# Layer norm in a two-layer encoder: statistics by products with a constant matrix of 1/D, and 1/std by square root, reciprocal and one Newton step

## The chip, the cores and the metric

The kernel runs on one core of a Trainium2 chip. The metric is device time in microseconds (us) of one execution. The core's engines run side by side, each through its own instructions in order: TensorE (PE in the profile: matmuls; PEld: its weight loads), VectorE (DVE), ScalarE (ACT), GpSimd (POOL) and SyncE (SP, which issues the DMAs here). An instruction that waits for another engine also holds back what stands behind it on its own engine.

## The reference

The program is two layers of a hybrid encoder over 1024 prompt tokens and 32 sample tokens, with D = 1024 features and a feed-forward width of 2816. Each layer has an input projection, mixers (pooling and a short convolution in layer 0, spatial gating and a state-space scan in layer 1), an output projection, and then three steps:

```python
x = layer_norm(alpha * x + mix, ln1_g, ln1_b)                                    # LN1
x = layer_norm(alpha * x + (silu(x @ w1) * (x @ w3)) @ w2, ln2_g, ln2_b)         # LN2
x = x + (ple[i] @ w_ple) * jax.nn.sigmoid(x @ w_gate)

def layer_norm(x, g, b, eps=1e-5):
    mu = jnp.mean(x, -1, keepdims=True)
    var = jnp.mean(jnp.square(x - mu), -1, keepdims=True)
    return (x - mu) * lax.rsqrt(var + eps) * g + b
```

All numbers are float32. The statistics of a layer norm are per token, over its 1024 features.

## The kernel before, in words

**Layout.** Activations lie with features on the 128 partitions: 8 blocks of 128 features by 1056 tokens (`stream`). A sum over features is therefore a sum over 8 blocks, which VectorE can do, and a sum over 128 partitions, which only a matmul does here. Tokens are cut in two ways: into three chunks of 384, 384 and 288 (named 0, 1, 2) or into two halves of 528 (t = 0, 1).

**Products.** Each big product is made of parts: an operand is split into a high part (`xhin`, `xhgate`; ScalarE, L323) and the rest (`xlin`, `xlgate`; VectorE, L324), and TensorE does three products, high by high, high by low and low by high (L228 to L230). From L990 on, and at L1203, a block-wise scheme with fewer products is used, on `quads` (PSUM tiles of two halves of 264 columns).

**Order.** Python code emits the work of each engine, and a list scheduler in the compiler then puts each engine's instructions in an order; at run time that order is fixed. To lay small steps under big products, the code calls `defer(us, fn)`: it counts the columns given to TensorE as time, and emits `fn` once that many microseconds of products have been passed. Those waits are the constants `LN_A` (before the first step of a norm), `LN_S` (between the two statistics), `LN_B` (before the result is applied), `LN_C` and `LN_D` (between the pieces in which it is applied).

**Where the norm stands.** `norm()` is called ten times, at two kinds of place.

- LN1, on chunks (`rows` is None), three times in each layer, in the function `tail` of a layer. The output projection (`down`: products L228 to L230, results added to `stream` by VectorE at L1282, `evacuate`) goes chunk by chunk. After every second feature block, `sums` squares that part (ScalarE) and adds it to S and Q (VectorE, L1394, L1395; at the end L1399): 128 partial sums of z and z*z for each token. When a chunk is done, its norm runs under the products of the next chunk; then it gives the chunk's operands `xhin` and `xlin`, in four pieces of two feature blocks. Behind chunk 2 of `down` the first products of the feed-forward (`up` of its first group, again L228 to L230, chunk after chunk, into `c`, L886) take these operands: they run while the norms of chunks 1 and 2 are still under way. After them the block-wise products at L990 begin.
- LN2, on halves (`rows` given), twice in each layer. t = 0 begins in the last products of the feed-forward (L1203) and lies under the 192 products with `w_ple` (L1310, whose results ScalarE copies out at L1315); these do not need its result. The gate's products (L1331, sigmoid at L1337) do need it: their operands `xhgate` and `xlgate` are this norm's output, in four pieces. t = 1 lies under the gate's products for t = 0.

**The norm itself.** `stats` multiplies S, as the stationary operand, 128 tokens at a time, by a column of 1/D (`rD`), and Q likewise: mean and mean square stand on the partitions, one token each, 3 or 5 columns (L1412). Small VectorE operations make the variance (L1425 to L1429). GpSimd raises it to the power -0.5 (L1430), multiplies the mean by the result (L1431), and builds diagonal matrices from both (`dg`, L1441). `spread` multiplies these by a matrix of ones (`cst`), so that 1/std and mean/std of every token stand on all partitions (L1456); on halves ScalarE copies them out of PSUM (L1468). Then, in each of four pieces, VectorE multiplies by 1/std (L1479) and subtracts mean/std (L1480), ScalarE applies gain and bias (L1482), and the piece is split (L323, L324).

Of the kernel before, what the change touches and what calls it, by code (L numbers as in the profile page):

```python
# [7 lines left out]
F32 = mybir.dt.float32  # L8
# [6 lines left out]
P = 128  # L15
# [18 lines left out]
LN_A, LN_B, LN_C, LN_D, LN_S = 4.0, 5.0, 2.0, 4.0, 1.0  # L34
# [164 lines left out]
class Kernel:  # L199
# [50 lines left out]
    def build(self):  # L250
        nc, tc, a = self.nc, self.tc, self.a
        with ExitStack() as ctx:
# [34 lines left out]
            self.rD = const.tile([P, 1], F32, name="rD")  # L287
            nc.vector.memset(self.rD, 1.0 / D)
# [979 lines left out]
    def norm2(self, layer, t):  # L1268

        tok = slice(t * TH, (t + 1) * TH)  # L1270
        x = [v[:, :, tok] for v in (self.xh, self.xl)]
        self.norm(
            2 * layer + 1, t, [self.row(i) for i in (0, 2)], self.stream[:, :, tok], x, TH, self.done2,
            0, [self.row(i) for i in (8, 10, 22, 23, 4, 6)],
        )
# [104 lines left out]
    def sums(self, ln, c, i, S):  # L1380
# [19 lines left out]
        return out[:, 0, :], Q[:, 0, :]  # L1400

    def norm(self, ln, c, S, acc, x, n, done, wait=LN_A, rows=None):

        nc, lp = self.nc, self.hp if rows else self.lp

        full = n // P
        tiles = [i * P for i in range(full)] + [n - P] * (n % P > 0)
        nt = len(tiles)

        def stats(st, i):  # L1410
            for j, o in enumerate(tiles):
                nc.tensor.matmul(  # L1412
                    st[:, nt * i + j:nt * i + j + 1], S[i][:, o:o + P], self.rD, start=True, stop=True
                )

        def first():
            st = self.quads()[:, 0, :] if rows else self.bank("ms")
            stats(st, 0)
            self.defer(LN_S, lambda: second(st))

        def second(st):
            stats(st, 1)
            sm = lp.tile([P, 2, nt], F32, tag="sm", name=f"sm{ln}_{c}", bufs=2)
            rn = lp.tile([P, 2, nt], F32, tag="rn", name=f"rn{ln}_{c}", bufs=2)
            nc.vector.tensor_copy(sm.rearrange("p a b -> p (a b)"), st[:, 0:2 * nt])  # L1425
            mean, var = sm[:, 0, :], sm[:, 1, :]
            nc.vector.tensor_tensor(rn[:, 0, :], mean, mean, op=ALU.mult)
            nc.vector.tensor_tensor(var, var, rn[:, 0, :], op=ALU.subtract)
            nc.vector.tensor_scalar(out=var, in0=var, scalar1=0.0, scalar2=EPS, op0=ALU.max, op1=ALU.add)  # L1429
            nc.gpsimd.tensor_tensor(rn[:, 0, :], var, self.mhalf[:, 0:nt], op=ALU.pow)  # L1430
            nc.gpsimd.tensor_tensor(rn[:, 1, :], mean, rn[:, 0, :], op=ALU.mult)  # L1431

            dg = []
            for i in range(2):
                for j in range(0, nt, 3):
                    k = min(3, nt - j)
                    if rows:
                        d = rows[len(dg) + 2][:, :k * P]
                    else:
                        d = lp.tile([P, 3 * P], F32, tag=f"dg{i}", name=f"dg{ln}_{c}_{i}", bufs=1)  # L1440
                    nc.gpsimd.tensor_tensor(  # L1441
                        d.rearrange("p (a t) -> p a t", a=k), self.ident.unsqueeze(1).to_broadcast([P, k, P]),
                        col(rn[:, i, j:j + k], P), op=ALU.mult,
                    )
                    dg.append(d)
            self.defer(LN_B, lambda: apply([dg[:len(dg) // 2], dg[len(dg) // 2:]]))

        def spread(ps, dg, t, end):

            t0 = t  # L1450
            while t < end:
                tail = t >= full * P
                j = full if tail else t // P
                upto = min(end, n if tail else min(full, j // 3 * 3 + 3) * P)
                o = t - tiles[j] + j % 3 * P
                nc.tensor.matmul(  # L1456
                    ps[:, t - t0:upto - t0], self.ones, dg[j // 3][:, o:o + upto - t], start=True, stop=True
                )
                t = upto

        def apply(dg):
            ab = []
            for i in range(2):
                if rows:
                    q = self.quads()
                    for a in range(2):
                        spread(q[:, a, :], dg[i], a * n // 2, (a + 1) * n // 2)
                    nc.scalar.activation(rows[i].rearrange("p (a t) -> p a t", a=2), q[:, :, :n // 2], AF.Copy)  # L1468
                    ab.append(rows[i])
                else:  # L1470
                    ps = self.bank("ms")
                    spread(ps, dg[i], 0, n)
                    ab.append(ps[:, :n])
            pieces([v.unsqueeze(1).to_broadcast([P, 2, n]) for v in ab], 0)

        def pieces(ab, k):
            ks = slice(k, k + 2)
            z = acc[:, ks, :]
            nc.vector.tensor_tensor(z, z, ab[0], op=ALU.mult)  # L1479
            nc.vector.tensor_tensor(z, z, ab[1], op=ALU.subtract)  # L1480
            for kk in (k, k + 1):
# [3 lines left out]
                )  # L1485
            self.split(x, ks, z)
            done[c] += 1
            if k + 2 < KD:
                self.defer(LN_D if rows else LN_C, lambda: pieces(ab, k + 2))
# [118 lines left out]
```

## Time and profile before

| | before |
|---|---|
| median of 3 runs | 2334.34 us (2331.43 to 2335.2) |
| the profiled execution | 2331.33 us |
| its span in the trace | 2329.6 us, granted TensorE clock 0.998 |
| TensorE busy | 2307.0 us, 99% of the span |
| VectorE busy | 1543.4 us, 66% |
| ScalarE busy | 966.1 us, 41% |
| GpSimd busy | 71.4 us, 3% |
| DMA | 207.37 MB moved, mean 89 GB/s |

The span is the time from the first to the last instruction in the trace; the profiled execution took 1.7 us more than that. Busy times add up the instructions of an engine; a busy TensorE still includes matmuls that wait in its pipeline. In the rows, `L1203 PE MATMUL q<-w 128*128 128x264 f32` is the instruction of line 1203 on TensorE that writes tile `q` from tile `w`, with its shapes; "x12" is how many, and in the chain of waits the numbers ahead are when a piece of the chain began and how long it lasted. Tile names are those under which a buffer was first made, and buffers are used again: `t1down` and `t2down` hold this norm's diagonals on halves, S and Q of a half among others, and `cst` holds the matrix of ones.

### The profile page before, as it was taken

The numbers are of one execution on the slowest core, as the hardware profiler recorded it, in microseconds if no ns is written. First come the engines' busy times: TensorE is split into PE (matmuls) and PEld (weight loads), VectorE is DVE, ScalarE is ACT, GpSimd is POOL, SyncE is SP. The second block draws the span as 40 slices with busy tenths as digits, with TensorE's granted clock in tenths as the row PEclk, the third lists the DMA queues.
The fourth block names the chain that finished last, engine by engine and source line by source line (L and its number), as shares of the span: only waits on it lengthen the run. The fifth ranks groups of instructions, "written<-read, shape, count | busy, mean of one in ns | idle before, by whom it ended". The sixth has DMA issues, their size and how long they took to land.

```text
span 2329.6 us, 41097 instructions
## 1 busy us (share of the span) xinstructions
PE 2307.0 (99%) x17567; PEld 2273.9 (98%) x17567; DVE 1543.4 (66%) x2426; ACT 966.1 (41%) x1616; POOL 71.4 (3%) x88
## 2 busy tenths in 40 slices
PE   9999999999999999999999999999999999999998
PEld 8999999999999999999999989999999999999998
DVE  8755787544554978775556774787554454978773
ACT  5432354333333444474543562353333333434462
POOL 0000000000000000100000120100000000000100
PEclk9999999999999999999999999999999999999999
DMA  4113123222224621124212222022222225521132
GB/s 148 47 55 127 39 68 107 74 83 74 92 73 151 239 88 44 46 83 141 80 38 66 100 85 61 19 89 94 84 73 89 73 69 205 215 69 42 37 102 91
DMA packets 84378, 207.37 MB, mean 89 GB/s; under 512 B 10236, under 2 KB 19652, under 8 KB 84196
## 3 DMA queue, kind: packets, MB, share of 16 engines
q1 hardware_dynamic: 83428, 204.07, 26.5%
q8 instruction: 137, 2.24, 0.4%
q10 hardware_dynamic: 768, 0.68, 0.1%
q14 instruction: 45, 0.37, 0.1%
HBM read 171.57 MB, written 33.16 MB: 88 GB/s over the span
## 4 chain that ended last, share of the span: by engine, by line
PE 94%; DVE 3%; DMA 1%; POOL 1%; ACT 1%; issue 0%; SPq 0%; POOLq 0%; ACTq 0%
PE q L990 38%; PE q L1203 20%; PE q L1331 8%; PE mm L228 6%; PE mm L229 6%; PE mm L230 6%; PE q L1310 2%; PE mm L639 1%; PE mm L640 1%; PE mm L641 1%; DVE bf L94 1%; PE ms L775 1%; DVE w L89 1%; DMA raw<-w_out 1%; DMA raw<-w 0%
## 5 line engine op out<-in xcount | busy, mean ns | idle before, releaser
L1203 PE MATMUL q<-w 128*128 128x264 f32 x3696 | 457.0, 285 | 0.0
L1203 PEld LDWEIGHTS q<-w 128*128 128x128 f32 x3696 | 456.1, 188 | 0.0
L88 ACT ACTIVATE w<-raw 128x512 fp32r<-128x512 f32 (+2 forms) x246 | 185.7, 774 | 221.1 <-issue 76.3
L990 PE MATMUL q<-xhin,w 128*128 128x264 f32 x1664 | 270.7, 284 | 2.0 <-ACT xhin L963 0.8
L89 DVE TENSOR_TENSOR w<-raw,w 128x512 fp32r<-128x512 f32 (+2 forms) x246 | 212.8, 878 | 55.1 <-ACT w L88 54.8
L89 DVE TENSOR_TENSOR w<-bf,w 128x512 fp32r<-128x512 f32 (+1 forms) x250 | 167.0, 691 | 106.7 <-ACT w L88 105.5
L990 PEld LDWEIGHTS q<-xhin,w 128*128 128x128 f32 x1664 | 230.1, 188 | 3.0 <-ACT xhin L963 1.0
L88 ACT ACTIVATE w<-bf 128x512 fp32r<-128x512 f32 (+1 forms) x250 | 149.0, 629 | 195.9 <-PE q L990 77.9
L990 PE MATMUL q<-xhgate,w 128*128 128x264 f32 x1280 | 207.9, 284 | 0.6 <-DVE c L886 0.6
L228 PE MATMUL mm<-xhgate,w 128*128 128x384 f32 (+1 forms) x576 | 187.5, 326 | 1.1 <-ACT xhgate L323 1.1
L230 PE MATMUL mm<-xlgate,w 128*128 128x384 f32 (+1 forms) x576 | 186.1, 324 | 0.0
L229 PE MATMUL mm<-xhgate,w 128*128 128x384 f32 (+1 forms) x576 | 185.9, 323 | 0.0
L990 PEld LDWEIGHTS q<-xhgate,w 128*128 128x128 f32 x1280 | 176.8, 188 | 1.0 <-issue 0.8
L990 PE MATMUL q<-xlin,w 128*128 128x264 f32 x832 | 169.9, 285 | 0.6 <-DVE xlin L964 0.6
L1331 PE MATMUL q<-xhgate,w 128*128 128x264 f32 x1024 | 166.7, 285 | 0.0
L1331 PEld LDWEIGHTS q<-xhgate,w 128*128 128x128 f32 x1024 | 141.6, 188 | 0.0
L990 PE MATMUL q<-xlgate,w 128*128 128x264 f32 x640 | 130.0, 285 | 0.4 <-DVE xlgate L964 0.4
L990 PEld LDWEIGHTS q<-xlin,w 128*128 128x128 f32 x832 | 128.8, 188 | 1.3 <-DVE xlin L964 1.0
L228 PE MATMUL mm<-xhin,w 128*128 128x384 f32 (+1 forms) x384 | 125.5, 328 | 3.0 <-ACT w L88 1.8
L229 PE MATMUL mm<-xhin,w 128*128 128x384 f32 (+1 forms) x384 | 124.2, 325 | 0.6 <-DVE w L89 0.6
L94 DVE TENSOR_TENSOR bf<-raw 128x512 f32<-128x512 f32 x50 | 34.5, 691 | 135.8 <-DMA raw<-w 129.8
L230 PE MATMUL mm<-xlin,w 128*128 128x384 f32 (+1 forms) x384 | 123.9, 325 | 0.0
(329 smaller groups left out, 4305.7 us busy)
## 6 DMA issues: line engine op xcount, KB each, us to landing
raw<-w SPq DMA_DIRECT2D x116, 512.0 KB, 3.6
hidden<-c SPq DMA_DIRECT2D x44, 528.0 KB, 3.0
raw<-w_gate SPq DMA_DIRECT2D x32, 512.0 KB, 3.6
raw<-w_in SPq DMA_DIRECT2D x16, 512.0 KB, 3.8
raw<-w_out SPq DMA_DIRECT2D x16, 512.0 KB, 3.6
xhdown<-hidden SPq DMA_DIRECT2D x12, 528.0 KB, 7.7
t2down<-hidden SPq DMA_DIRECT2D x8, 528.0 KB, 3.8
t3down<-hidden SPq DMA_DIRECT2D x8, 528.0 KB, 3.9
```

The source lines that it names most:

```text
L88: self.nc.scalar.activation(hi, x, AF.Copy)
L89: self.nc.vector.tensor_tensor(lo, x, hi.bitcast(F32), op=ALU.subtract)
L94: self.nc.vector.tensor_tensor(t, a, b, op=op)
L228: nc.tensor.matmul(ps, wh, xh, start=first, stop=False)
L229: nc.tensor.matmul(ps, wl, xh, start=False, stop=False)
L230: nc.tensor.matmul(ps, wh, xl, start=False, stop=last)
L639: nc.tensor.matmul(o, xh, hi[:, s], start=k == 0, stop=False)
L640: nc.tensor.matmul(o, xh, lo[:, s], start=False, stop=False)
L990: nc.tensor.matmul(ps[:, a, :TH // 2], w[q][:, ks], x[r][:, k, a * TH // 2:(a + 1) * TH // 2], start=not add and k == 0 and j == 0, stop=k ...
L1203: nc.tensor.matmul(ps[m][:, a, :TH // 2], v[q][:, ms], x[r][:, a * TH // 2:(a + 1) * TH // 2], start=j == 0 and n == 0, stop=j == NG - 1 a ...
L1310: nc.tensor.matmul(ps[:, b, :TH // 2], w[q][:, o:o + P], pe[k][r][:, t * TH + b * TH // 2:t * TH + (b + 1) * TH // 2], start=k == 0 and i ...
L1331: nc.tensor.matmul(ps[:, b, :TH // 2], w[q][:, ks], token_half((self.xh, self.xl), k, t, b)[r], start=k == 0 and i == 0, stop=k == KD - 1 ...
```

## The change

What changes:

- The matrix of ones is multiplied once, at the start, by 1/D. A product of it with S or Q then gives the mean, or the mean square, of each token on every partition at once (`average`). On chunks it is one product of 384 or 288 columns for each of the two, on halves two products of 264 columns for each.
- ScalarE copies the mean out of PSUM and squares it (L1431, L1432 of the new code). VectorE makes the variance (L1437, L1438), now 128 partitions by 384, 288 or 528 elements, ScalarE takes the square root (L1439, with a load of its table of functions), VectorE the reciprocal (L1444), and a Newton step follows: square (ScalarE, L1445), times the variance (VectorE, L1451), times -0.5 plus 1.5 (ScalarE, L1452), times the reciprocal (VectorE, L1457).
- The mean is subtracted from the four pieces of z in between (VectorE, L1427), before the multiplication by 1/std (L1463); each piece still has two VectorE operations for this, a gain and bias (L1465), and a split (L322, L323). `LN_B`, which stood once in a norm with 5.0, now stands three times with 2.0.
- GpSimd has no part in it any more: the power, the mean/std and the diagonals are gone, and so are the small statistics products and the products that spread them.

```diff
-LN_A, LN_B, LN_C, LN_D, LN_S = 4.0, 5.0, 2.0, 4.0, 1.0
+LN_A, LN_B, LN_C, LN_D, LN_S = 4.0, 2.0, 2.0, 4.0, 1.0
...
-            self.rD = const.tile([P, 1], F32, name="rD")
-            nc.vector.memset(self.rD, 1.0 / D)
+            nc.vector.tensor_scalar(out=self.ones, in0=self.ones, scalar1=1.0 / D, scalar2=None, op0=ALU.mult)
...
-        return out[:, 0, :], Q[:, 0, :]
+        return out, Q
...
+        if rows:
+            mean, var, inv, tmp = (r[:, :n] for r in rows[:4])
+        else:
+            mean, inv = (
+                lp.tile([P, 384], F32, tag=f"dg{i}", name=f"dg{i}_{ln}_{c}", bufs=2)[:, :n] for i in range(2)
+            )
+            var, tmp = S[0][:, 1, :], S[0][:, 0, :]
+
+        def average(v):
+            v = v if rows else v[:, 0, :]
+            if not rows:
+                ps = self.bank("ms")
+                nc.tensor.matmul(ps[:, :n], self.ones, v, start=True, stop=True)
+                return ps[:, :n], lambda t: t
+            q, h = self.quads(), n // 2
+            for a in range(2):
+                nc.tensor.matmul(q[:, a, :h], self.ones, v[:, a * h:(a + 1) * h], start=True, stop=True)
+            return q[:, :, :h], lambda t: t.rearrange("p (a t) -> p a t", a=2)
+
+        def minus(k):
+            z = acc[:, k:k + 2, :]
+            nc.vector.tensor_tensor(z, z, mean.unsqueeze(1).to_broadcast([P, 2, n]), op=ALU.subtract)
 
         def first():
-            st = self.quads()[:, 0, :] if rows else self.bank("ms")
-            stats(st, 0)
-            self.defer(LN_S, lambda: second(st))
...
-            nc.gpsimd.tensor_tensor(rn[:, 0, :], var, self.mhalf[:, 0:nt], op=ALU.pow)
-            nc.gpsimd.tensor_tensor(rn[:, 1, :], mean, rn[:, 0, :], op=ALU.mult)
...
+            ps, cut = average(S[0])
+            nc.scalar.activation(cut(mean), ps, AF.Copy)
+            nc.scalar.activation(cut(tmp), ps, AF.Square)
+            self.defer(LN_S, second)
+
+        def second():
+            ps, cut = average(S[1])
+            nc.vector.tensor_tensor(cut(var), ps, cut(tmp), op=ALU.subtract)
             nc.vector.tensor_scalar(out=var, in0=var, scalar1=0.0, scalar2=EPS, op0=ALU.max, op1=ALU.add)
+            nc.scalar.activation(tmp, var, AF.Sqrt)
+            minus(0)
+            self.defer(LN_B, third)
+
+        def third():
+            nc.vector.reciprocal(inv, tmp)
+            nc.scalar.activation(tmp, inv, AF.Square)
+            minus(2)
+            self.defer(LN_B, fourth)
+
+        def fourth():
 
+            nc.vector.tensor_tensor(tmp, tmp, var, op=ALU.mult)
+            nc.scalar.activation(tmp, tmp, AF.Copy, scale=-0.5, bias=1.5)
+            minus(4)
+            self.defer(LN_B, fifth)
+
+        def fifth():
+            nc.vector.tensor_tensor(inv, inv, tmp, op=ALU.mult)
+            pieces(0)
+
+        def pieces(k):
             ks = slice(k, k + 2)
             z = acc[:, ks, :]
-            nc.vector.tensor_tensor(z, z, ab[0], op=ALU.mult)
-            nc.vector.tensor_tensor(z, z, ab[1], op=ALU.subtract)
+            nc.vector.tensor_tensor(z, z, inv.unsqueeze(1).to_broadcast([P, 2, n]), op=ALU.mult)
...
+            if k == 0:
+                minus(6)
```

Below are two places at which the order of the instructions changes. A row names line, operation, tiles (with the number of their buffer) and shape. Elsewhere, outside the norms, every engine runs the same instructions in the same order, except that ScalarE has 46 loads of its function table in place of 33, for the square roots among its other functions.

TensorE in layer 0, at the end of the feed-forward (L1203) and the start of the `w_ple` products (L1310), where the norm of half t = 0 stands. Before, the ten small statistics products (`rD`) come first, and after three groups of `w_ple` products TensorE comes to the eight products that spread 1/std (from `t1down`) and mean/std (from `t2down`):

```order
L1412 MATMUL q_10109<-rD,t2down_7482 128x1 x5
L1203 MATMUL q_9782<-w_10008 128x264 x6
L1203 MATMUL q_9782<-w_10037 128x264 x6
L1310 MATMUL q_10168<-c0p,w_10078 128x264 x6
L1310 MATMUL q_10168<-w_10071,w_10078 128x264 x6
L1310 MATMUL q_10182<-c0p,w_10078 128x264 x6
L1310 MATMUL q_10182<-w_10071,w_10078 128x264 x6
L1310 MATMUL q_10196<-c0p,w_10078 128x264 x6
L1310 MATMUL q_10196<-w_10071,w_10078 128x264 x6
L1456 MATMUL q_10209<-t1down_7550,cst 128x264
L1456 MATMUL q_10209<-t1down_7550,cst 128x120
```

The same place of the changed kernel, where lines of the code are numbered one less:

```order
L1422 MATMUL q_10085<-t2down_7458,cst 128x264 x2
L1202 MATMUL q_9757<-w_9984 128x264 x5
L1202 MATMUL q_9757<-w_10013 128x264 x6
L1422 MATMUL q_10102<-t2down_7458,cst 128x264 x2
L1202 MATMUL q_9758<-w_9984 128x264 x6
L1202 MATMUL q_9758<-w_10013 128x264 x6
L1309 MATMUL q_10133<-c0p,w_10054 128x264 x6
L1309 MATMUL q_10133<-w_10047,w_10054 128x264 x6
L1309 MATMUL q_10150<-c0p,w_10054 128x264 x6
L1309 MATMUL q_10150<-w_10047,w_10054 128x264 x6
```

The four products that average stand where the statistics stood, among the last products of the feed-forward, and no product among those with `w_ple` belongs to the norm any more.

VectorE in the tail of layer 0, while TensorE does chunk 2 of `down`. Before, the norm of chunk 0 hands out its last operands (`xlin`), chunk 2 is taken in (L1282, L1394, L1395), and the norm of chunk 1 starts on its pieces with its 1/std and mean/std read from PSUM (`ms`):

```order
L1282 TENSOR_TENSOR stream<-stream,mm_2781 128x288
L1394 TENSOR_TENSOR S_2_1_2740<-S_2_1_2740,stream 128x2x288
L1395 TENSOR_TENSOR Q_2_0_2683<-Q_2_0_2683,sq_2_2_2777 128x2x288
L324 TENSOR_TENSOR xlin<-stream,xhin 128x2x384
L1479 TENSOR_TENSOR stream<-stream,ms_2808 128x2x384
L1282 TENSOR_TENSOR stream<-stream,mm_2795 128x288
L1480 TENSOR_TENSOR stream<-stream,ms_2810 128x2x384
L1394 TENSOR_TENSOR S_2_1_2740<-S_2_1_2740,stream 128x2x288
```

The same stretch of the changed kernel; `dg_0_1_2637` is the mean of chunk 1, `dg_0_1_2638` its 1/std, and `dg_0_0_2491` the 1/std of chunk 0:

```order
L1393 TENSOR_TENSOR S_2_1_2721<-stream 128x2x288
L1394 TENSOR_TENSOR Q_2_0_2674<-Q_2_0_2674,sq_2_1_2719 128x2x288
L1463 TENSOR_TENSOR stream<-stream,dg_0_0_2491 128x2x384
L1444 RECIPROCAL dg_0_1_2638<-S_1_1_2562 128x384
L323 TENSOR_TENSOR xlin<-stream,xhin 128x2x384
L1427 TENSOR_TENSOR stream<-stream,dg_0_1_2637 128x2x384
L1281 TENSOR_TENSOR stream<-stream,mm_2738 128x288
L1281 TENSOR_TENSOR stream<-stream,mm_2764 128x288
L1393 TENSOR_TENSOR S_2_1_2721<-S_2_1_2721,stream 128x2x288
L1394 TENSOR_TENSOR Q_2_0_2674<-Q_2_0_2674,sq_2_2_2760 128x2x288
L1463 TENSOR_TENSOR stream<-stream,dg_0_0_2491 128x2x384
L1451 TENSOR_TENSOR S_1_1_2562<-S_1_1_2562 128x384
```

Chunk 1's reciprocal, subtraction and Newton product now stand between the last two pieces of chunk 0, ahead of chunk 0's last operands and of the intake of chunk 2 (L1281).

More of the change, by code (lines that the diff above doesn't have):

```diff
@@ L1273, in norm2 @@
             2 * layer + 1, t, [self.row(i) for i in (0, 2)], self.stream[:, :, tok], x, TH, self.done2,
-            0, [self.row(i) for i in (8, 10, 22, 23, 4, 6)],
+            0, [self.row(i) for i in (8, 10, 4, 6)],
         )
@@ L1399, in sums @@
             nc.vector.tensor_tensor(v[:, 0, :], v[:, 0, :], v[:, 1, :], op=ALU.add)
-        return out[:, 0, :], Q[:, 0, :]
+        return out, Q
     def norm(self, ln, c, S, acc, x, n, done, wait=LN_A, rows=None):
         nc, lp = self.nc, self.hp if rows else self.lp
[L1406 to L1414, printed above, removed]
@@ L1416, in first @@
-        def first():
-            st = self.quads()[:, 0, :] if rows else self.bank("ms")
-            stats(st, 0)
-            self.defer(LN_S, lambda: second(st))
[L1421 to L1428, printed above, removed]
-            nc.vector.tensor_scalar(out=var, in0=var, scalar1=0.0, scalar2=EPS, op0=ALU.max, op1=ALU.add)
-            nc.gpsimd.tensor_tensor(rn[:, 0, :], var, self.mhalf[:, 0:nt], op=ALU.pow)
-            nc.gpsimd.tensor_tensor(rn[:, 1, :], mean, rn[:, 0, :], op=ALU.mult)
[L1433 to L1474, printed above, removed]
@@ L1476, in pieces @@
-        def pieces(ab, k):
+        if rows:
[15 more added lines that the diff above has]
+            return q[:, :, :h], lambda t: t.rearrange("p (a t) -> p a t", a=2)
@@ L1488, in pieces @@
             if k + 2 < KD:
-                self.defer(LN_D if rows else LN_C, lambda: pieces(ab, k + 2))
+                self.defer(LN_D if rows else LN_C, lambda: pieces(k + 2))
         self.defer(wait, first)
```

## The prediction

> **What bounds the kernel now.** I read the busy line of the page first, then the chain of waits, then TensorE's waits by releaser.
>
> ```profile
> PE 2307.0 (99%) x17567; PEld 2273.9 (98%) x17567; DVE 1543.4 (66%) x2426; ACT 966.1 (41%) x1616; POOL 71.4 (3%) x88
> PE 94%; DVE 3%; DMA 1%; POOL 1%; ACT 1%; issue 0%; SPq 0%; POOLq 0%; ACTq 0%
> PE ms L1456 <- POOL dg L1441: 2.7, 4, 1.0
> PE q L1456 <- POOL t1down L1441: 2.0, 2, 1.0
> PE q L1456 <- POOL t2down L1441: 1.3, 2, 0.6
> ```
>
> TensorE sets the time: it is busy for 99% of the span. The chain leaves it for GpSimd in 1%, and the last three rows (idle us of TensorE, times, longest) are its waits for the norm's diagonals. The change can therefore gain only where TensorE does products for the norm or waits for it, and lose only where it makes TensorE wait. I look at the two kinds of place apart. First the chain at LN2 of layer 0 (start, length), then two rows of layer 1:
>
> ```profile
> 975.61 1.22 PE q L1412 x10
> 978.29 1.01 PE q L1412 x10
> 983.02 2.02 POOL rn L1430
> 985.41 1.86 POOL t1down L1441 x2
> 987.27 2.29 POOL t2down L1441 x2
> 989.61 0.62 PE q L1456 x4
> 990.22 19.05 PE q L1310 x156
> 1015.13 1.01 PE q L1412 x10
> 1022.09 1.01 PE q L1412 x10
> 1029.05 2.14 PE q L1456 x16
> 2204.76 20.99 PE q L1310 x156
> 2225.75 5.86 PE q L1331 x48
> ```
>
> TensorE has done three groups of `w_ple` products when it comes to the spreading ones, and waits there for GpSimd's power and diagonals; then 156 undisturbed products take 19.05 us, 0.1221 each. Layer 1 needs 20.99 us for the same 156. The windows show why (length, busy and count for PE, PEld, DVE, ACT, POOL, then granted clock, DMA share, GB/s):
>
> ```profile
> 980.86:1009.27 28.41, 26.55 (x211) 25.74 (x210) 23.96 (x24) 22.22 (x34) 6.45 (x6) 1.00 0.18 57
> 2194.79:2225.75 30.96, 29.21 (x210) 28.44 (x209) 23.92 (x24) 22.14 (x34) 6.50 (x6) 0.89 0.17 52
> 2205.00:2210.00 5.00, 5.00 (x28) 5.00 (x28) 5.00 (x5) 1.82 (x4) 0.00 (x0) 0.61 0.01 2
> ```
>
> The first two run from the first `w_ple` product to the first gate product. In layer 1 the clock is 0.89 over the stretch and 0.61 in the 5 us behind the wait. The second kind of place, the tail of layer 0: windows from the start of chunk 0's norm to chunk 0's last operand (292.65), to chunk 1's (316.34), and from there to the end of the first `up` products; then rows of TensorE and VectorE.
>
> ```profile
> 255.45:292.65 37.20, 35.83 (x228) 33.88 (x227) 30.71 (x49) 18.36 (x24) 6.00 (x8) 1.00 0.10 29
> 255.45:316.34 60.89, 58.28 (x357) 55.59 (x356) 49.86 (x78) 28.08 (x39) 8.62 (x12) 1.00 0.14 44
> 316.34:339.40 23.06, 22.55 (x153) 22.32 (x151) 22.57 (x38) 15.90 (x30) 0.00 (x0) 1.00 0.14 47
> 267.27 1.29 PE ms L1456 x4
> 283.71 1.42 PE ms L1412 x12
> 314.11 1.17 PE ms L1456 x6
> 290.59 0.91 PE L1456 MATMUL ms<-dg,cst 128*128 128x384 f32 x2 [0.98 <-POOL dg L1441]
> 291.89 0.91 PE L1456 MATMUL ms<-dg,cst 128*128 128x384 f32 x2 [0.39 <-POOL dg L1441]
> 297.95 0.44 PE L228 MATMUL mm<-xhin,w 128*128 128x384 f32 x1 [1.12 <-ACT xhin L323]
> 339.53 0.73 PE L990 MATMUL q<-xhin,w 128*128 128x264 f32 x4 [0.64 <-DVE c L886]
> ```
>
> Here VectorE is nearly as full as TensorE: 49.86 of 60.89 us, then 22.57 of 23.06. Its 11.0 us of idle time up to 316.34 are all the cover there is for new VectorE work; what exceeds it reaches TensorE, which takes its operands `xhin` and `xlin` from this queue. And at 339.53 TensorE waits for VectorE's `c` (0.64 us).
>
> **LN2, t = 0.** 192 `w_ple` products at 0.1221 us are 23.45 us. The stretch takes 28.41 us in layer 0 and 30.96 in layer 1, so 4.96 and 7.51 us of it are waits, spreading products and lost clock. None of these has a cause left: the order shows no product of the norm among the `w_ple` ones. I keep 0.3 us for a wait for a free PSUM tile: −4.7 and −7.2. The statistics (1.22 + 1.01 = 2.23 us) become four products of 264 columns. Their price is that of the same product with `cst`, 1.29 us for 4 x 192 columns, so 1056 columns cost 1.77: −0.45 per layer.
>
> **LN2, t = 1.** Statistics and spreading, 1.01 + 1.01 + 2.14 = 4.16 us on the chain, become 1.77: −2.4 per layer. Together LN2 gives −(4.7 + 7.2 + 0.9 + 4.8) = −17.6 us.
>
> This holds if the gate's operands come in time, since the norm's critical queue is now VectorE. The prices:
>
> ```profile
> L671 DVE RECIPROCAL sp_s<-sp_s 128x72 f32<-128x72 f32 x1 | 0.6, 603 | 0.0
> 1000.33 1.25 DVE L324 TENSOR_TENSOR xlgate<-stream,xhgate 128x1056 fp32r<-128x1056 f32 x1
> 1014.65 1.22 DVE L89 TENSOR_TENSOR w<-raw,w 128x1024 fp32r<-128x1024 f32 x1
> 1016.56 0.71 DVE L1338 TENSOR_TENSOR bf<-bf,t2down 128x528 f32<-128x528 f32 x1
> 275.21 0.55 DVE L1399 TENSOR_TENSOR S<-S 128x384 f32<-128x384 f32 x1
> 1014.62 1.28 ACT L1337 ACT_TABLE_LOAD   x1
> 1015.91 0.61 ACT L1337 ACTIVATE bf<-q 128x528 f32<-128x528 f32 x1
> ```
>
> The disputed one is the reciprocal on wide tiles, which the trace has only at 72 elements: 603 ns, 8.4 ns each. If time goes with the elements, 384 cost 3.2 us, 288 cost 2.4 and 528 cost 4.4; the other end is an ordinary operation of 384, 0.55 us. I take 3.2, because 603 ns for 72 elements already exceeds what 384 cost there. [...] Ordinary operations I count by the step from one to the next, some 0.08 us under their rows: 0.46 for 384 elements, 0.37 for 288, 0.87 for 768.
>
> Walking VectorE's new order from the first `w_ple` product: one add 0.6, three weight splits 3.4, reciprocal 4.4, two subtractions 2.3, two Newton products 1.2, six operations for half 1's sums 3.7, four multiplications 4.7, four `xlgate` 4.7, two more of 528 1.2: 26.2 us, plus 0.6 for the start and 1 of waits for ScalarE, 27.8. The last `xlgate` is needed when TensorE has done the `w_ple` products and three quarters of a gate group, about 28.7; the earlier pieces come at 19.9, 21.7 and 26.0, needed at 24.2, 25.7 and 27.2. So it is hidden with about 1 us to spare, and exposed if that cover is gone. ScalarE, 22 of 28 us busy there, gets four passes of 528 (0.61 each) and a table load of 1.28, and loses two copies of half the norm: it fits. The 13 further loads cost 13 x 1.28 = 17 us of an engine that is busy for 41%, on the path only in a norm's own round trip. The product ones x 1/D at the start waits for a DMA that lands before VectorE gets there, and nothing is behind it: 0.
>
> **LN1, the tails.** TensorE gains, per layer: three sets of statistics (1.42 each; the averages of chunks 0 and 1 cost what spreading cost, 1.29, so only these go), 0.35 on chunk 2 (1.31 for spreading 288 columns twice with its split, against 768 to 576 columns of 1.29, 0.96), and the waits for GpSimd, 0.98 + 0.39: 4.6 + 1.4 = 6 us.
>
> VectorE gets, per layer: reciprocals 3.2 + 3.2 + 2.4 = 8.8; variance 0.46 + 0.46 + 0.37 = 1.3; maximum and epsilon 1.1; two Newton products for each chunk, 2.6: 13.8 us. It loses fifteen small operations (0.08 each, 1.2) and the slowing beside GpSimd:
>
> ```profile
> 265.00 1.62 POOL L1441 TENSOR_TENSOR dg<-cst,rn 128x384 f32<-128x384 f32 x2
> 265.79 1.63 DVE L1394 TENSOR_TENSOR S<-S,stream 128x768 f32<-128x768 f32 x1
> 272.61 0.94 DVE L1394 TENSOR_TENSOR S<-S,stream 128x768 f32<-128x768 f32 x1
> ```
>
> The same operation takes 1.63 us while GpSimd builds diagonals and 0.94 alone; three such operations in a tail give back 2.0. Net +10.6 us for VectorE in a stretch with 11.0 idle, of which not all can be filled.
>
> By the order, chunk 0's last operand has more ahead of it than its own norm. Summed by steps, VectorE's work up to it was 28.0 us (the 30.71 hold overlaps and the slowing), now it is 41.0: two reciprocals 6.5 (chunk 1's stands ahead too), variances, maxima and Newton products of two chunks 3.1, three of chunk 1's subtractions 2.6, a weight split and an add moved ahead 1.5, less 0.6 of small operations. With 2.3 to 4 us of idle time (6.5 before; some of it waits for data) it comes at 255.45 + 43.3 to 45 = 299 to 300.4, 7 us late. TensorE, with its savings, gets there at about 290.5 and waits some 9 us. That isn't lost whole, since more of the products around it are done before the wait: the bound moves to VectorE for this stretch. Up to chunk 1's last operand the work rises from 46.9 by steps to 61.4; with the same idle time it comes at 319 to 321 in place of 316.34. Behind it stand 46 products of 384 columns (by columns from 0.1221 for 264, 0.178 each: 8.2 us) and 96 of 288 (0.133: 12.8), so L990 begins at 340 to 342.5 in place of 339.53; I take 342, since TensorE already waited for VectorE at the end. The bounds: 0, if the idle time fills, and +5, if the clock falls behind the stall as it did in layer 1's LN2 (1.9 us there). I take +2.5 per layer, +5 for both: TensorE's own 6 us go into the wait, and something on top.
>
> **Sum.** −17.6 + 5 = −12.6 on the profiled execution's 2331.3 gives 2318.7; that execution lies 3.0 under the median of 2334.3, so 2321.7 for the median, say 2322.
>
> **The rivals.** The measurement cannot tell less than 0.2%, 4.7 us, from no change.
> - *The tails gain as well.* VectorE's idle time takes in all the new work, or the reciprocal is cheap; TensorE keeps its 6 us per layer. For it: 11.0 us idle against +10.6. Against it: the order, with chunk 1's reciprocal ahead of chunk 0's operands. −17.6 − 12 is 2305. Chance 0.15.
> - *The gate waits.* VectorE's walk is 1 us too long already, or a table load falls in each round trip, and half of LN2's gain at t = 0 (6 us) goes, or all of it, with the tails as above: 2327 to 2335. For it: 1 us of slack in 28. Chance 0.18, of which 0.08 faster and 0.10 the same.
> - [...] Chance 0.06, faster. [...]
> - *Slower: VectorE hands all of its new work to TensorE.* Place: the tails. Each chunk's norm has three round trips to ScalarE that the list scheduler cannot fill (0.5 us each, 4.5 for three chunks, from the rows of 0.55 and 0.61), and the 10.6 us come on top: +15.1 per layer, 30 − 17.6 = +12.6, 2347. It decides from +8.8 per layer (LN2's gain used up), and measurably from 11.1. Against it: 11.0 us of idle time there. Chance 0.11: 0.09 slower, 0.02 the same.
>
> **How the numbers follow.** The forecast itself, 2317 to 2328, has 0.50, all faster. Faster: 0.50 + 0.15 + 0.08 + 0.06 = 0.79; the same 0.10 + 0.02 = 0.12; slower 0.09. The range takes in the forecast, the table, the gate's wait and the near part of the gain in the tails: 2308 to 2335. It leaves out the slower case and the far part of the first rival.
>
> **What would show it.** LN2: no GpSimd in the chain; the stretch from the first `w_ple` to the first gate product at about 23.8 us in both layers, with the clock at 1.00 in layer 1; no wait of the gate for `xlgate`. Tails: the reciprocal at 3.2 us for 384 elements; TensorE waiting some 9 us for `xhin` or `xlin` of chunk 0 in the first `up`; L990 beginning 2 to 3 us late against the start of the norm. Wrong would make it a reciprocal far from 3.2, a tail that moves by more than 5 us, or the gate waiting.

## The result and the profile after

The changed kernel takes 2315.74 us (median of 6 runs, 2314.35 to 2317.23) against 2332.89 (6 runs, 2328.19 to 2337.43): ratio 0.9927, 95% interval 0.9913 to 0.9941, some 17 us faster. Its profiled execution has a span of 2313.8 us against 2329.6. First the page's busy line and its chain by engine:

```profile
PE 2290.7 (99%) x17375; PEld 2257.9 (98%) x17375; DVE 1572.1 (68%) x2436; ACT 1001.5 (43%) x1671; POOL 32.4 (1%) x40
PE 91%; DVE 5%; DMA 2%; ACT 1%; issue 1%; POOL 0%; SPq 0%; ACTq 0%; POOLq 0%
```

All of TensorE's waits that come to over 1 us, from the list of waits (total us, times, longest):

```profile
PE mm L228 <- ACT xhin L322: 5.5, 2, 4.4
PE mm L228 <- ACT xhgate L322: 4.7, 2, 4.4
PE mm L372 <- DVE u L382: 1.4, 1, 1.4
```

GpSimd has 0% of the chain and no row in the waits. In its place TensorE waits, twice in each layer, for ScalarE's `xhin` (in layer 1 the same buffer is named `xhgate`); before, it did so once in each, for 1.1 us. VectorE has 29 us more work, ScalarE 35, and TensorE 16 us less.

The 17319 products outside the norm are the same in both kernels, so the start of each can be set against its partner. Their order is the same too but for 8 in the first 70 us and some 120 in each tail; on VectorE and ScalarE as well, splits and additions beside the norms have moved, so more changed place than the two stretches ahead of the prediction show. The bounds of the stretches lie outside the moved products. By stretch, change of duration in us, from the two traces:

| stretch of TensorE (times of before) | predicted | measured |
|---|---|---|
| start to 253 (before the first tail) | 0 | −0.69 |
| tail, layer 0 (253 to 339.53) | +2.5 | +0.16 |
| LN2 layer 0: statistics | −0.45 | −0.46 |
| LN2 layer 0: `w_ple` products (980.7 to 1009.1) | −4.7 | −4.64 |
| LN2 layer 0: t = 1 | −2.4 | −2.66 |
| end of layer 0 (1107): a new wait | 0 | +0.96 |
| tail, layer 1 (1470 to 1554.7) | +2.5 | +0.18 |
| feed-forward, layer 1 (1554.7 to 2189) | 0 | +1.94 |
| LN2 layer 1: statistics, `w_ple`, t = 1 | −0.45, −7.2, −2.4 | −0.46, −7.26, −2.66 |
| the rest | 0 | −0.2 |
| sum | −12.6 | −15.8 |

The new wait at the end of layer 0, in TensorE's timeline (start, length, and in brackets the idle time before and who ended it):

```profile
1099.43 0.44 PE L228 MATMUL mm<-xhgate,w 128*128 128x384 f32 x1 [0.70 <-ACT bf L1336]
```

The first product of layer 1 waits 0.70 us for ScalarE's last sigmoid of the gate. The wait stands in the trace of every kernel below with the new norm on halves, and in none with the old one; why the order brings it there is not shown.

LN2 in the windows that the prediction showed of before: from the first `w_ple` product to the first gate product, in both layers.

```profile
979.47:1003.24 23.77, 23.61 (x194) 23.40 (x193) 23.63 (x24) 21.05 (x32) 0.00 (x0) 1.00 0.19 67
2188.61:2212.39 23.78, 23.62 (x194) 23.41 (x193) 23.64 (x24) 21.06 (x32) 0.00 (x0) 1.00 0.20 68
```

23.8 us in both, clock 1.00, where 28.41 and 30.96 stood; VectorE (the third of the busy numbers, 23.63) is full. The tail of layer 0, TensorE's two waits in the timeline:

```profile
288.47 0.44 PE L228 MATMUL mm<-xhin,w 128*128 128x384 f32 x1 [1.10 <-ACT xhin L322]
295.81 0.69 PE L228 MATMUL mm<-xhin,w 128*128 128x384 f32 x1 [4.44 <-ACT xhin L322]
```

VectorE's timeline around them:

```profile
285.24 0.96 DVE L1463 TENSOR_TENSOR stream<-stream,dg 128x768 f32<-128x768 f32 x1
286.11 2.56 DVE L1444 RECIPROCAL dg<-S 128x384 f32<-128x384 f32 x1
288.57 0.91 DVE L323 TENSOR_TENSOR xlin<-stream,xhin 128x768 fp32r<-128x768 f32 x1
...
292.31 0.96 DVE L1463 TENSOR_TENSOR stream<-stream,dg 128x768 f32<-128x768 f32 x1
296.01 0.97 DVE L323 TENSOR_TENSOR xlin<-stream,xhin 128x768 fp32r<-128x768 f32 x1
```

And two windows there:

```profile
285.00:295.00 10.00, 5.18 (x27) 4.22 (x25) 10.00 (x14) 5.05 (x9) 0.00 (x0) 0.96 0.00 0
295.00:301.00 6.00, 5.19 (x15) 4.81 (x16) 6.00 (x9) 3.11 (x5) 0.00 (x0) 0.50 0.27 87
```

Chunk 0's last two pieces are multiplied by 1/std at 285.24 and 292.31; between them stands chunk 1's reciprocal and more. VectorE is busy for 10.00 of 10 us while TensorE does 5.18, and behind the wait TensorE has half its clock: 0.50 in the window from 295 to 301, and by the record of the granted clock from 294.12 to 300.95, 6.83 us.

### The profile page after: what moved, and what is told of

It reads as the page before. It is cut to its first block, busy times and chain, and to the rows that moved or that the text cites. A ratio compares the mean times of both kernels' runs of the same rounds, so it can differ in the third digit from the quotient of the medians.

```text
span 2313.8 us, 40696 instructions
## 1 busy us (share of the span) xinstructions
PE 2290.7 (99%) x17375; PEld 2257.9 (98%) x17375; DVE 1572.1 (68%) x2436; ACT 1001.5 (43%) x1671; POOL 32.4 (1%) x40
## 3 DMA queue, kind: packets, MB, share of 16 engines
q8 instruction: 136, 2.23, 0.4%
## 4 chain that ended last, share of the span: by engine, by line
PE 91%; DVE 5%; DMA 2%; ACT 1%; issue 1%; POOL 0%; SPq 0%; ACTq 0%; POOLq 0%
PE q L989 37%; PE q L1202 20%; PE q L1330 8%; PE mm L228 6%; PE mm L229 6%; PE mm L230 6%; PE q L1309 2%; PE mm L638 1%; PE mm L639 1%; PE mm L640 1%; DVE bf L94 1%; DMA raw<-w 1%; DVE w L89 1%; PE ms L774 1%; DMA raw<-w_out 1%
## 5 line engine op out<-in xcount | busy, mean ns | idle before, releaser
L1330 PE MATMUL q<-xhgate,w 128*128 128x264 f32 x1024 | 167.1, 285 | 0.0
L1330 PEld LDWEIGHTS q<-xhgate,w 128*128 128x128 f32 x1024 | 142.0, 188 | 0.3
L989 PE MATMUL q<-t2sum,w 128*128 128x264 f32 x960 | 124.2, 285 | 0.0
```

The costliest lines, as they stand in the source:

```text
L989: nc.tensor.matmul(ps[:, a, :TH // 2], w[q][:, ks], x[r][:, k, a * TH // 2:(a + 1) * TH // 2], start=not add and k == 0 and j == 0, stop=k ...
L1330: nc.tensor.matmul(ps[:, b, :TH // 2], w[q][:, ks], token_half((self.xh, self.xl), k, t, b)[r], start=k == 0 and i == 0, stop=k == KD - 1 ...
```

## The experiments

Eleven kernels, each timed beside the kernel before, whose median was 2330.17 us beside the first four of them, 2333.31 beside the next four and 2329.44 beside the last three (2332.89 beside the full change): between groups, the ratios compare, not the medians. The columns on the tails hold two numbers, for layer 0 and layer 1. "Tails" is the change of duration against the kernel before, measured as in the table above. "Idle" is how long TensorE stands idle in the tail, and "half clock" how long its granted clock is 0.50 there, part of it while TensorE waits.

| kernel | median us | ratio to before, 95% interval | tails | idle | half clock |
|---|---|---|---|---|---|
| the kernel before | | | 0, 0 | 3.25, 3.12 | 0, 0 |
| the full change | 2315.74 | 0.9927 (0.9913 to 0.9941) | +0.16, +0.18 | 5.77, 5.50 | 6.83, 6.83 |
| new norm on halves only | 2316.04 | 0.9935 (0.9923 to 0.9946) | −0.14, +0.38 | 3.12, 3.20 | 0, 0 |
| new norm on chunks only | 2331.5 | 1.0 (0.9991 to 1.0008) | +0.41, −0.47 | 5.77, 5.51 | 6.83, 3.41 |
| chunks: copy for reciprocal | 2308.39 | 0.9906 (0.9892 to 0.992) | −4.25, −4.23 | 2.50, 2.23 | 3.41, 3.41 |
| halves: reciprocal twice | 2322.52 | 0.9962 (0.9949 to 0.9974) | −0.17, −0.53 | 5.77, 5.51 | 6.83, 3.41 |
| chunks: longer reciprocal | 2321.66 | 0.9958 (0.9945 to 0.9971) | +0.91, +1.38 | 5.81, 6.22 | 6.83, 6.83 |
| chunks: ln and exp | 2312.24 | 0.9916 (0.9903 to 0.993) | −2.47, −1.59 | 5.28, 5.87 | 0, 0 |
| chunks: shorter waits | 2318.3 | 0.994 (0.9928 to 0.9953) | +1.43, +0.71 | 7.05, 6.31 | 6.83, 3.41 |
| chunks: ln and exp, shorter waits | 2318.57 | 0.9944 (0.9931 to 0.9958) | +3.40, +1.77 | 7.34, 6.78 | 10.24, 6.83 |
| chunks: no Newton step | 2319.7 | 0.9959 (0.9947 to 0.9972) | −0.78, −0.96 | 4.92, 5.07 | 6.83, 3.41 |
| chunks: ln and exp, no Newton step | 2307.76 | 0.9909 (0.9894 to 0.9924) | −4.12, −3.89 | 4.13, 2.28 | 0, 3.41 |
| halves new; chunks old, diagonals by ScalarE | 2306.69 | 0.9902 (0.9889 to 0.9916) | −4.55, −3.75 | 0, 0 | 0, 0 |

**Which half of the change carries the time.** The old and the new `norm` stand side by side, with a second matrix of ones/D.

```diff
 # halves only (from the kernel before)
-        self.norm(2 * layer + 1, t, ..., [self.row(i) for i in (8, 10, 22, 23, 4, 6)])
+        self.norm_new(2 * layer + 1, t, ..., [self.row(i) for i in (8, 10, 4, 6)])
 # chunks only (from the changed kernel)
-        self.norm(2 * layer + 1, t, ..., [self.row(i) for i in (8, 10, 4, 6)])
+        self.norm_old(2 * layer + 1, t, ..., [self.row(i) for i in (8, 10, 22, 23, 4, 6)])
```

> New norm on the halves (LN2) alone, the chunks (LN1) as before. Theory 1 (LN2 carries all of the gain; in the two traces the steps at LN2 sum to -17.3 us and the tails give +0.7): 2333 - 17 = 2316 us, ratio 0.992 to 0.994, no wait of TensorE for GpSimd outside the tails, no clock window at half speed in LN2. Rival (the chunks carry a good part, by TensorE's 6 us less work and waiting in each tail): 2322 to 2327.

> New norm on the chunks (LN1) alone, the halves (LN2) as before. Theory 1: +0.7 us against before, ratio 0.999 to 1.002, with a wait of some 4.4 us of TensorE for xhin in each tail and half the clock for 6.8 us behind it. Rival: -6 to -12 us, ratio 0.995 to 0.9975.

Halves alone give the whole gain, within the intervals, and chunks alone none. The waits of the chunks-only kernel, from its list:

```profile
PE mm L229 <- ACT xhin L326: 5.5, 2, 4.4
PE mm L229 <- ACT xhgate L326: 4.7, 2, 4.4
PE q L1538 <- POOL t1down L1523: 2.0, 2, 1.0
PE q L1538 <- POOL t2down L1523: 1.3, 2, 0.6
```

Two windows of it, behind the waits for GpSimd in LN2 of layer 0 and of layer 1:

```profile
990.00:995.00 5.00, 4.37 (x23) 4.14 (x22) 4.97 (x5) 2.40 (x4) 1.76 (x2) 0.66 0.02 6
2205.00:2210.00 5.00, 4.00 (x25) 3.40 (x26) 4.93 (x5) 2.13 (x4) 3.42 (x4) 1.00 0.22 83
```

The tail has the waits of the full change, LN2 those of before. The windows hold a surprise: behind the same waits the clock fell in layer 0 here (0.66) and not in layer 1 (1.00), the other way round than in the profile of before. The layer 1 stretch was 2.63 us shorter than there, so this much of its 7.26 was a clock drop that the same code does not always have.

**Is it VectorE's work that sets the tail?** The chunks' reciprocal becomes a copy:

```diff
-            nc.vector.reciprocal(inv, tmp)
+            if rows:
+                nc.vector.reciprocal(inv, tmp)
+            else:
+                nc.vector.tensor_copy(inv, tmp)
```

> The full change with the chunks' reciprocal (2.55, 2.55 and 1.95 us) replaced by a copy of the same shape (estimated 0.3 to 0.5): 1/std is not computed on the chunks, the work around it is. Takes some 6 us of VectorE out of each tail. Theory 1 (VectorE's work in the tail sets when chunk 0's operands come, TensorE waits for it and loses clock behind the wait): the wait of 4.4 us falls to under 1.5, no half clock, 4 to 6 us less in each tail, 2304 to 2308 us. Rival (the round trips to ScalarE and the order set it, not VectorE's work): 2313 to 2316, the wait stays over 3 us.

TensorE's waits in the first tail, in the timeline:

```profile
287.35 0.45 PE L228 MATMUL mm<-xhin,w 128*128 128x384 f32 x1 [0.22 <-ACT xhin L322]
292.37 0.44 PE L228 MATMUL mm<-xhin,w 128*128 128x384 f32 x1 [2.29 <-ACT xhin L322]
```

The wait falls from 4.44 to 2.29 us, each tail gains 4.4 us, and the median misses the expected range by 0.4 us. More is left than was expected: 2.29 us of wait in place of under 1.5, and half the clock in both tails where none was expected. Two windows of it:

```profile
293.30:296.60 3.30, 3.30 (x13) 3.30 (x12) 3.30 (x6) 1.38 (x2) 0.00 (x0) 0.50 0.55 159
1498.20:1501.50 3.30, 3.30 (x12) 3.30 (x12) 3.30 (x7) 1.15 (x2) 0.00 (x0) 0.50 0.50 159
```

TensorE is idle for 3.3 us less in each tail; most of the rest of the 4.4 goes with the shorter half clock. What the copy cannot tell apart is VectorE's queue and the norm's own chain from S to 1/std: the reciprocal stands in both, and the copy shortens both.

**Slack in LN2.** One more line, `if rows: nc.vector.reciprocal(inv, tmp)`, behind the reciprocal.

> The full change with the reciprocal on halves done twice, 3.45 us more of VectorE in each of the four norms on halves. Theory 1 with about 1 us of slack for the gate's last operand at t = 0: TensorE waits 2 to 2.5 us for xlgate in each layer, 2319 to 2322 us, more if the clock falls behind it. Rival (the slack is over 3.5 us): no change, 2315 to 2317.

The gate's first product in layer 0, in the timeline:

```profile
1007.47 0.75 PE L1330 MATMUL q<-xhgate,w 128*128 128x264 f32 x4 [1.64 <-ACT t3down L1314]
```

And the gate's waits in its list of waits:

```profile
PE q L1330 <- ACT t3down L1314: 3.3, 2, 1.6
PE q L1330 <- DVE xlgate L323: 0.6, 1, 0.6
```

The gate does wait, but in the main not for the operand that the expectation named: its first product waits 1.64 us for ScalarE to copy out the last `w_ple` results (L1314), which stand behind the norm's gains and splits in ScalarE's order. In the trace 3.45 us more cost 1.35 us at t = 0 in each layer and 1.05 to 1.35 at t = 1, 5.1 in all: the slack at t = 0 is 2.1 us. Its median, 2322.52, is 0.5 above the expected range; in its trace the clock also fell to half at 9.30 and 1268.82, for 3.41 us each, outside the edit.

**The price of the reciprocal.** Chunks get a second one over a quarter of the columns (`nc.vector.reciprocal(inv[:, :n // 4], tmp[:, :n // 4])`).

> The full change with a second reciprocal over a quarter of the columns on chunks, which brings the reciprocal from the measured 2.55 and 1.95 us to the 3.2 and 2.4 of the prediction. Theory 1 (the prediction sized the tails too dear by the reciprocal's price): each tail 1.4 us worse than in the full change, +3 us in all, 2317.5 to 2320. Rival (the price isn't what was wrong, the tail takes that much in without loss): 2315 to 2317.

The second one takes 0.74 us for 96 elements and 0.60 for 72. The tails lose 0.75 and 1.2 us against the full change, 2.0 together where 2.8 were expected. The median is higher than that accounts for (2321.66, runs from 2319.27 to 2325.25): these runs were granted a clock of 0.994 to 0.997, the lower the longer the run, and those of the full change 0.997 to 0.998. So with about the price that the prediction assumed the tails would stand at +0.9 and +1.4, still under its +2.5.

**Ln and exp for square root and reciprocal**, on chunks, where the reciprocal goes as well:

```diff
-            nc.scalar.activation(tmp, var, AF.Sqrt)
+            nc.scalar.activation(tmp, var, AF.Ln)
+            nc.scalar.activation(inv, tmp, AF.Exp, scale=-0.5)
```

> The full change with the chunks' square root and reciprocal replaced by exp(-0.5 ln x) on ScalarE: no reciprocal on VectorE (2.55 + 2.55 + 1.95 us less in a tail), one more pass and up to two more table loads of 1.28 us on ScalarE for each chunk. Theory 1 (VectorE's work sets the tail): near the kernel with a copy for the reciprocal, 2306 to 2311 us. Rival (ScalarE's loads take the place of the reciprocal on the round trip): 2313 to 2318.

The first waits in this kernel's tail of layer 0, in the timeline:

```profile
290.26 0.44 PE L228 MATMUL mm<-xhin,w 128*128 128x384 f32 x1 [2.25 <-ACT xhin L322]
294.61 0.44 PE L228 MATMUL mm<-xhin,w 128*128 128x384 f32 x1 [1.46 <-ACT xhin L322]
```

The median lies between the two ranges, and the tails gain 2.6 and 1.8 us, not 4.4. But TensorE is idle for as long as in the full change, 5.28 and 5.87 us, in more and shorter waits. What is gained comes with the clock, which did not fall in either tail: in the full change some 5.1 us of products run at half clock in each, worth up to 2.6 us (an estimate from the end of the wait, 295.81, to the end of the half clock, 300.95). So the waits fit the rival: VectorE has 7 us less to do, but ln and exp stand on ScalarE in the chain of a chunk's norm in the reciprocal's place, with the loads of their tables by the author's estimate (a load of the full change took 1.28 us); what these loads cost in this kernel is not shown.

**Is it the order?** Same instructions, other times at which they are emitted (on chunks, `defer` takes `LN_BC` in place of `LN_B` at its three places):

```diff
+LN_BC = 1.0          # on chunks, for LN_B
-LN_C = 2.0
+LN_C = 1.0
```

> The full change with other waits on chunks: 1.0 in place of 2.0 us of products between the steps of the norm, and between the pieces. Same instructions; in VectorE's order chunk 0's last operand has some 10 us less work ahead of it, chunk 1's last 4 us less. Theory 2 (it is not the amount of VectorE's work alone but what stands ahead of chunk 0's operands that makes TensorE wait): no wait over 1 us for xhin in the tails, no half clock there, 3 to 5 us less in each tail, 2306 to 2310 us. Theory 1 in its plain form (the sum of VectorE's work to the end of the tail sets it): under 2 us in each, 2312 to 2316.

> Both: exp(-0.5 ln x) on ScalarE for the chunks, and the shorter waits. Theory 1 and 2 together: TensorE keeps all of its 6 us less work and waiting in each tail, 2303 to 2306 us. Rival (ScalarE now sets the tail): 2308 to 2315.

Theory 2 fell, for these two orders, and both medians lie above both of their ranges. TensorE's long wait in the tail of layer 0, in the timeline of the kernel with shorter waits alone:

```profile
301.44 0.69 PE L229 MATMUL mm<-xhin,w 128*128 128x384 f32 x1 [4.64 <-ACT xhin L323]
```

And in that of the kernel with ln and exp and shorter waits:

```profile
300.61 0.44 PE L230 MATMUL mm<-xhin,w 128*128 128x384 f32 x1 [4.50 <-DVE w L90]
```

Chunk 0's operands come in time now, and TensorE waits as long as in the full change, 4.64 us, for the first operand of chunk 1; with ln and exp it waits 4.50 us for a weight split (L90) that VectorE was given late. Both kernels also wait for the sums S and Q ahead of averaging, for up to 1.23 us, and 2.31 with ln and exp. What is drawn forward pushes something else back: in these two orders the wait moved and TensorE's idle time grew. That no order does better is not shown.

**Without the Newton step**, on chunks: the two `tensor_tensor` and two `activation` lines get `if rows:`.

> The full change without the Newton step on chunks: two products of VectorE (2.6 us in a tail) and two passes of ScalarE less for each chunk, so that 1/std has the precision of the square root's table. Theory 1 (VectorE's work in the tail is handed to TensorE): 1.5 to 2.5 us less in each tail, 2311 to 2313 us. Rival (only the reciprocal, ahead of chunk 0's operands, counts): 2315 to 2316.

> exp(-0.5 ln x) on ScalarE for the chunks, and no Newton step on chunks either: 9.7 us less of VectorE in a tail than in the full change. Theory 1: TensorE keeps nearly all of its 6 us per tail, 2306 to 2309 us. Rival (the table loads on ScalarE set it now): 2311 to 2313, as with the Newton step.

The longest wait in the tail of layer 0, in the timeline of the kernel with the reciprocal:

```profile
297.50 0.69 PE L229 MATMUL mm<-xhin,w 128*128 128x384 f32 x1 [4.32 <-DVE w L89]
```

And with ln and exp:

```profile
289.94 0.44 PE L228 MATMUL mm<-xhin,w 128*128 128x384 f32 x1 [1.76 <-ACT xhin L322]
```

The first misses both of its ranges: less work on VectorE, and still a wait of 4.32 us, for a weight split again, in another order of the scheduler's. Its tails gain only 0.9 to 1.1 us against the full change, and its ratio is worse (0.9959 against 0.9927). In its trace that loss lies outside the tails: 2.6 us more in the first 253 us, 1.6 between 1107 and 1470, and 1.3 in the feed-forward of layer 1. Two windows show what most of the first two is:

```profile
8.87:12.28 3.41, 3.41 (x11) 3.41 (x12) 3.41 (x4) 2.78 (x4) 0.00 (x0) 0.50 1.07 378
1264.98:1268.39 3.41, 3.41 (x16) 3.35 (x15) 0.57 (x3) 0.26 (x1) 0.00 (x0) 0.50 0.55 165
```

The clock fell to half at both places, worth up to 1.7 us each (an estimate, half of 3.41), and in the full change's trace at neither. So this median says little about the Newton step, and the tails say more. The second kernel's tails gain 4.3 and 4.1 us against the full change, 1.6 and 3.2 of it idle time, and its median is in the expected range.

**A version that beats both.** Halves new, chunks old, but with the diagonals made by ScalarE:

```diff
-                    nc.gpsimd.tensor_tensor(
-                        d.rearrange("p (a t) -> p a t", a=k), self.ident.unsqueeze(1).to_broadcast([P, k, P]),
-                        col(rn[:, i, j:j + k], P), op=ALU.mult,
-                    )
+                    for a in range(k):
+                        nc.scalar.activation(
+                            d[:, a * P:(a + 1) * P], self.ident, AF.Copy, scale=rn[:, i, j + a:j + a + 1]
+                        )
```

> New norm on halves, old norm on chunks, but with the diagonals on chunks built by ScalarE (18 passes of 128 columns in a tail) in place of GpSimd, which keeps the power and one small product. VectorE's operations are no longer slowed beside GpSimd (2 us in a tail). Theory 1: the waits of 1.0 and 0.4 us for the diagonals shrink, VectorE has slack, 1 to 3 us less in each tail than with GpSimd's diagonals (2316): 2310 to 2314. Rival (the passes on ScalarE are no sooner done): 2315 to 2317.

Two windows from the start of the tail of layer 0:

```profile
255.00:292.00 37.00, 37.00 (x239) 35.87 (x238) 29.55 (x50) 20.99 (x36) 2.33 (x4) 1.00 0.12 33
255.00:315.00 60.00, 60.00 (x375) 58.69 (x374) 48.18 (x78) 33.70 (x57) 3.38 (x6) 1.00 0.14 44
```

ScalarE's timeline, one of the three sets of diagonals there:

```profile
288.54 1.87 ACT L1445 ACTIVATE dg<-cst,rn 128x128 f32<-128x128 f32 x6
```

TensorE is busy for 60.00 of 60 us, and has no idle time in either tail. ScalarE builds a set of diagonals no faster than GpSimd did: 1.87 us, against the 1.62 of the row in the prediction. But GpSimd's set slowed VectorE beside it (1.63 us for an addition that takes 0.94 alone), and here no such addition (L1397, L1398) takes over 0.96. Of the 4.55 us that the tail of layer 0 gains, 3.25 are TensorE's idle time of before; the rest is spread over the products beside those waits. 2306.69 us is the shortest median (2306.08 to 2307.67), more of a gain than was expected, though TensorE keeps its old statistics products here; the intervals of the kernel with the copy, which leaves the reciprocal out, and of ln and exp without the Newton step overlap with its own.

## Why the prediction was right, and where its size was off

*LN2.* Forecast −17.6 us, −18.1 in the traces, of which the wait at the end of layer 0, which the prediction did not have, takes 0.96 back. Each part of the sum came out: the `w_ple` stretch at 23.8 us in both layers, the statistics at −0.46 for −0.45, t = 1 at −2.66 for −2.4. The gate's operands were hidden, as the walk through VectorE's order said; the slack is 2.1 us, where about 1 was forecast, and what comes late first is ScalarE's copy behind the norm's gains in its order, which the walk had waved through. That 7.2 us for layer 1 fits so well is partly luck: it was the price of one execution, and 2.6 of it depended on where the clock fell.

*The tails.* This term was mis-sized: +2.5 a layer forecast, +0.16 and +0.18 measured. The mechanism is there (VectorE full, TensorE waiting for chunk 0's operands, its 6 us used up), the step that failed is the sum of VectorE's work: chunk 0's last operand came at 296.98, which is 297.7 in the times of the before trace, in place of 299 to 300.4, chunk 1's at 316.87, or 317.6, in place of 319 to 321, and TensorE waited 4.44 + 1.10 us in place of 9. Part of that is the price of the reciprocal, in the view of its line (min, median and max in ns):

```profile
L1444 DVE RECIPROCAL dg<-S x6: 1952/2550/2555, 264.7 to 1520.4; 128x384 f32<-128x384 f32 x4, 128x288 f32<-128x288 f32 x2
L1444 DVE RECIPROCAL t2down<-t2down x4: 3447/3449/3458, 983.4 to 2231.6; 128x528 f32<-128x528 f32 x4
```

And of the maximum with epsilon, in the timeline:

```profile
262.40 0.36 DVE L1438 TENSOR_SCALAR S<-S 128x384 f32<-128x384 f32 x1
```

2.55 us, not 3.2; the maximum with epsilon took 0.27 by the step to the next, not 0.37. The kernel with the longer reciprocal puts the reciprocal's price at 1.0 us a tail of the 2.3 by which the forecast missed. The rest is idle time of VectorE that was filled better than the prediction allowed; how much each part of its sum contributed is not shown. The miss is larger than 2.3, for a second thing hides in the +0.16: in layer 0 TensorE's idle time rose by 2.5 us, half the clock behind the wait cost up to 2.6 (an estimate, as above), and the products that it no longer does saved some 4.9, in layer 1 nearly the same. The clock drop the prediction had only as a bound, so two errors in part cancel in the total. Two kernels with the same code in the tail show what the drop is worth: with 3.41 us of half clock in layer 1 in place of 6.83, that tail stands at −0.53 and −0.47.

*The rivals.* That the tails gain as well did not happen in this kernel; it happens in the kernel with the copy. The gate did not wait: no wait of its products (L1330) stands in the list. The one on the slower side, VectorE handing all of its work on, would have been +15 a tail; what was handed on is 0.2 us and the 6 that TensorE was to save. The chance of 0.06, and "the table" in the range, stand for a second cost beside each load of ScalarE's function table; no run shows such a term. In the traces of before and after, a function that waited for no other engine began 1.29 to 1.41 us after the start of its load of 1.28 us; in the tail the load at 262.84 is followed by its function at 264.13. But the load waits there for the function's data, and so lies on the norm's path. ScalarE's timeline:

```profile
262.84 1.28 ACT L1439 ACT_TABLE_LOAD   x1 [1.61 <-DVE S L1438]
264.13 0.52 ACT L1439 ACTIVATE S<-S 128x384 f32<-128x384 f32 x1
```

*Open.* The layer 1 feed-forward, whose code is the same, took 1.9 us more in the profile after. Between 1580 and 1600 it is 0.6, with a wait of 0.52 us for ScalarE's `xhgate` (L962). Another 1.4 us is spread evenly over the products from 1600 to 1960, 0.4% on each stretch of 20 us, without a wait and at a clock of 1.00. Eight of the other traces have 1.4 us or more there too; those of halves only, chunks only and diagonals by ScalarE, which keep the matrix of ones beside one of 1/D, have none. What slows these products is not shown.

## What to carry to other kernels

Moving work off the engine that bounds a stretch paid here only where the engine that took it was not waited for, and how full that engine is did not tell this alone. VectorE was 82% busy in the tail, where the change returned nothing, and 84% busy (23.96 of 28.41 us) under the `w_ple` products, where it was worth 12 us: those products do not need the norm's result, and 2.1 us of slack were left, while the next products of the tail take the norm's operands at once. If reordering moves a wait from one operand to another, look at the sum of the idle time: here two other orders raised it, and taking work off VectorE lowered it clearly only where the norm's own chain did not grow in exchange. In these kernels small diagonals on a ScalarE that had room (33.70 us busy of 60) beat both wide arithmetic on VectorE and diagonals on GpSimd. A stall's price in one profile includes what the clock did behind it (2.63 of 7.26 us in LN2 of layer 1), so check it against a second execution before it goes into a sum.

## What was not expected of the hardware

The reciprocal's time was a fixed part and a part by elements: 1.952, 2.550 and 3.449 us for 288, 384 and 528 elements are 6.24 ns each plus 0.155 us, and that line gives the 603 ns of the 72-element row too. Scaling one small row by its elements made 8.4 ns of it.

The granted clock fell to 0.50 at some waits and not at others, and their length does not tell which: waits of 3.6 to 5.6 us in the tails all came with a clock of 0.50, those of 2.2 to 2.3 us in the copy kernel too, a wait of 3.31 us in layer 1's tail of the ln and exp kernel with none, and the waits of 1.0 and 0.6 us in LN2 with a drop in one layer or the other. The time at 0.50 in a tail came to 0, 3.41, 6.83 or 10.24 us, and in the trace without the Newton step a drop of 3.41 us came at 1264.98 with no wait of 0.9 us or more ahead of it for over 900 us. What sets off a drop, and how long it lasts, is not explained by these runs.
